# A decode layer on one core: the order of issue from a first pass that follows every operand, sample tokens and transposes as streams of their own, weight halves in two steps

## The chip, the cores and the metric

The kernel runs on one core of a Trainium2 chip. Such a core has a matrix engine (TensorE, "PE"), a vector engine (VectorE, "DVE"), a scalar engine (ScalarE, "ACT"), a general one (GpSimd, "POOL") and a queue for transfers (SyncE, "SP"). Each engine works through its own list of instructions in order; between engines they wait on semaphores. The metric is the device time of one execution in microseconds (us), the median of several runs.

## The reference

One layer of a hybrid decoder, in fp32, for 16 meta tokens and 256 prompt tokens of one sequence, and for 8 sample sequences of 4 tokens each that continue from stored states. Cut to its core:

```python
z = rms_norm(x, norm_mix) @ w_in                       # 2048 -> 3360 + 4096 columns
z_a, z_b = z[..., :RWKV_COLS], z[..., RWKV_COLS:]
o_a, S_a = rwkv7_mixer(z_a, shifted z_a, S_a0, ...)    # 16 heads of 64
o_b, S_b = retention_mixer(z_b, S_b0, pos, prompt)     # 4 heads of 256, chunks of 128
h = x + concat(o_a, o_b) @ w_out                       # 2048 -> 2048
hn = rms_norm(h, norm_ffn)
h = h + (silu(hn @ w_gate) * (hn @ w_up)) @ w_down     # 2048 -> 5632 -> 2048
y = rms_norm(h, norm_final)
```

Inside `rwkv7_mixer` each head runs a recurrence over the tokens:

```python
sa = einsum('bhij,bhj->bhi', S, a_t)
S = S * w_t[:, :, None, :] + sa[..., None] * b_t[:, :, None, :] + v_t[..., None] * k_t[:, :, None, :]
out = einsum('bhij,bhj->bhi', S, r_t)
```

Outputs are `y` for prompt and samples, and the new states.

## The kernel before

**Main work.** All weights lie in one array `big`, packed in the order of use, and come as tiles `wr` of 1024 columns (512 KB) over SP's queue, up to `WR` = 4 tiles ahead. A weight of fp32 is split on the chip in two halves of type fp32r: `halve` (line 540) lets ACT cast 512 columns to `wh` and DVE subtract it from the raw weight to give `wl`. For each block of 128x128 weights, `main` (line 552) issues three matmuls into one `acc` bank: `wh` with the activations' upper half `xh`, `wh` with their lower half `xl`, and `wl` with `xh`. One pair of halves thus feeds four such triples, 12 matmuls. There are two `acc` banks, and `WS` = 4 buffers for each half; halves are made up to three groups of 512 columns ahead of use. When a job's last matmul is issued, `evacuate` reads the bank. `main` runs through the projections of the RWKV pairs and retention heads, then out projection and FFN.

**Streams.** Beside `main` run generators that each stand for a chain of work, with a `yield` wherever the chain has to wait for another engine. For each of the 8 pairs of heads there is `pair` (line 817): decays, normalisation, the products of a unit of 64 tokens, then `inverse` (line 1000, it inverts a triangular matrix per unit), `units` (line 1080, the recurrence over the 5 units) and `pair_out`. Two smaller generators were stepped from within these: `by_token` (line 976, transposes of tiles to token-major form) inside `inverse`, and `sample` (line 1132, the tokens of the 8 sample sequences) inside `units`, each by a `next(other, None)` at places written out by hand. `ret` does a head of retention. All their matmuls go to the other six PSUM banks, named `mm`; all their scratch tiles lie in one SBUF array that the profile calls `arena_dt.float`.

`inverse` is a substitution in 15 rounds. A round s has one STREAM_SHUFFLE on DVE that spreads row s (tile `rs`, 128x80), and a multiply and an add on POOL over the columns that are left, 5 x (15 - s).

**What sets the order.** Every instruction goes through a proxy that books it with a planner (so nearly all rows of the profile have line 300). The planner keeps a clock for each engine and, for each stream, a time `ready`. It picks the first stream whose time has come, else one block of `main`:

```python
at = max(self.clock[eng], self.ready) + dur
self.clock[eng] = at
self.end = max(self.end, at + lat)
```

A stream's next step is ready when the last one, `end`, is over; what its operands wait for beyond that isn't followed. The kernel is built twice. The first pass (`draft`) notes when each scratch tile is used first and last, counted in instructions; `Room.place` (line 426) then packs them into the arena, so that a tile may take the place of one whose last use lies more than `slack` instructions back, with the largest slack of 40, 20, 10, 5, 0 that fits. The second pass decides the order anew and issues. After it, a compiler's scheduler may still move instructions of one engine past each other.

Of the kernel before, what the change touches and what calls it, by code (L numbers as in the profile page):

```python
# [304 lines left out]
class Plan:  # L305
# [4 lines left out]
    def __init__(self, nc, rooms, draft):  # L310
        self.rooms, self.draft, self.count = rooms, draft, 0
        self.clock = dict(PE=0.0, DVE=0.0, ACT=0.0, POOL=0.0)
        self.ready = self.end = 0.0
        self.mode, self.parts, self.empty, self.begun = None, {}, 0.0, 0.0
# [5 lines left out]
        self.sp = Timed(self, nc.sync, "SP")  # L320

    def book(self, eng, what, a, k):
        self.count += 1
        if self.draft:
            for x in (*a, *k.values()):
                for room in self.rooms.values():
                    room.use(x, self.count)
        if eng == "SP":
            return
        free = lambda ap: math.prod(ap.shape[1:])  # L330
        if eng == "PE":
            self.array(what, *a[:3])
            return
        else:
            n = free(a[0])
            fixed, per, lat = {"DVE": (60, 1.05, 100), "ACT": (190, 0.84, 150), "POOL": (100, 2.2, 100)}[eng]
            dur = fixed + per * n
        at = max(self.clock[eng], self.ready) + dur
        self.clock[eng] = at
        self.end = max(self.end, at + lat)  # L340

    def array(self, what, out, w, x):
# [4 lines left out]
        mode, part = (up(k), up(m)), (w.start_partition(), out.start_partition())  # L347
        if w.dtype == F32R:
            mode = up(k), 128
            dur = max(0.417 * n + 12, 107)  # L350
        elif what == "transpose":
            dur = max(0.83 * n + 4, 60)
        else:
            dur = 2 * max(0.833 * n + 3, 58 if m <= 64 else 110)
        if mode != self.mode:
            self.mode, self.parts, self.empty = mode, {}, self.clock["PE"] + 90
        at = max(self.parts.get(part, self.empty), self.ready, self.begun + 5)
# [3 lines left out]
        self.end = max(self.end, self.clock["PE"] + 250)  # L361
# [6 lines left out]
    def pick(self, now):  # L368

        return next((s for s in self.streams if s[2] <= now), None)  # L370

    def step(self, s):
        self.ready, self.end = s[2], s[2]
# [6 lines left out]
    def run(self, main):  # L380

        over = False
        while self.streams or not over:
            now = self.clock["PE"]
            s = self.pick(now)
            if s is None and not over:
                self.ready = self.end = 0.0
                try:
                    if next(main):
                        continue  # L390
                except StopIteration:
                    over = True
                    continue
            if s is None:
                assert self.streams, "nothing left to wait for"
                s = min(self.streams, key=lambda s: s[2])
            self.step(s)

    def finish(self, gen):

        self.ready = self.end = 0.0
        while True:
            try:
                next(gen)
                self.ready = self.end
            except StopIteration as e:
                return e.value
# [64 lines left out]
class Step:  # L472


    def __init__(self, tc, I, O, ctx, rooms, draft):
# [8 lines left out]
        self.n = 0  # L484
        self.plan = pl = Plan(self.nc, rooms, draft)
# [4 lines left out]
        self.pe, self.dve, self.act, self.pool = pl.pe, pl.dve, pl.act, pl.pool  # L490
        self.outs = []
# [7 lines left out]
    def flush(self, all=False):  # L499
        while self.outs and (all or self.outs[0][0] <= self.plan.clock["PE"]):  # L500
# [1175 lines left out]
```

## Time and profile before

| | us |
|---|---|
| median of 3 runs (lowest, highest) | 1585.04 (1582.96, 1585.89) |
| the profiled execution's own time | 1582.62 |
| its span, first to last instruction | 1580.8 |
| ACT casts `wh<-wr`, 826 of them, busy | 509.5 |
| DVE subtractions `wl<-wr,wh`, 826, busy | 571.3 |
| PE matmuls into `mm`, 1072, busy | 171.9 |
| waits of PE right before those | 19.3 |

The times are of one profiled execution. A busy time counts an engine's instructions without the gaps; a wait stands beside the instruction that came after it, with the engine and the tile that it was put down to. The page divides the span into 40 slices of 39.5 us; POOL is at work in the first 16 of them only, in which the streams run, and the clock granted to PE has its digit at 9 in all of them. Matmuls overlap in the pipeline, so that the duration of one in a row (300 to 390 ns) is longer than the distance from its start to the next one's.

### The profile page before, as it was taken

The page shows a single profiled execution, that of the slowest core. Times are in us where ns is not written, and L with a number is a line of the kernel's source. Part 1 is how long each engine was busy: PE and PEld are TensorE (multiplying, and loading weights), DVE is VectorE, ACT ScalarE, POOL GpSimd, SP SyncE. Part 2 cuts the span into 40 slices and gives each one's busy share as a digit, 9 for nine tenths or more (in the row PEclk, how much of TensorE's full clock was granted, in tenths as well). Part 3 has the DMA queues.
Part 4 walks back from the last instruction along what each step waited for, and adds up shares of the span by engine and source line. Part 5 has one row for each costly group of instructions (what it writes and reads, how often), then busy time and mean ns, then how long its engine had stood idle before and what let it go on. Part 6 is the DMA issues. An engine that isn't in the chain of part 4 may idle for free.

```text
span 1580.8 us, 30987 instructions
## 1 busy us (share of the span) xinstructions
PE 1544.1 (98%) x11388; PEld 1510.5 (96%) x11388; DVE 1125.7 (71%) x2590; ACT 842.7 (53%) x1795; POOL 182.5 (12%) x567
## 2 busy tenths in 40 slices
PE   9999999999999999999999999999999999999997
PEld 8989899998988989999999999999999999999997
DVE  7888789887997877776565656666666666565657
ACT  6756777577766556365444444444444444444445
POOL 1463314513143000000000000000000000000000
PEclk9999999999999999999999999999999999999999
DMA  7543344334544547755555555555555555555553
GB/s 280 152 126 108 102 121 138 118 102 126 181 131 139 168 161 231 241 162 160 166 167 165 169 163 171 162 171 161 169 165 166 168 163 171 162 172 162 169 163 114
DMA packets 77000, 252.50 MB, mean 160 GB/s; under 512 B 9392, under 2 KB 14640, under 8 KB 76848
## 3 DMA queue, kind: packets, MB, share of 16 engines
q1 hardware_dynamic: 76848, 250.52, 51.0%
q8 instruction: 90, 1.47, 0.4%
q14 instruction: 62, 0.51, 0.1%
HBM read 236.21 MB, written 14.28 MB: 158 GB/s over the span
## 4 chain that ended last, share of the span: by engine, by line
PE 68%; ACT 1%; DVE 1%; DMA 0%; issue 0%; POOL 0%; DVEq 0%; ACTq 0%; POOLq 0%
PE acc L300 64%; PE mm L300 4%; ACT arena_dt.float L300 1%; DVE arena_dt.float L300 1%; DMA arena_dt.float<-s0r 0%; DVE wl L300 0%; ACT wh L300 0%; ACT arena_dt.float32r L300 0%; POOL arena_dt.float L300 0%; DVEq L1672 0%; DVE arena_dt.float32r L300 0%; ACTq L300 0%; DVEq L300 0%; POOLq L300 0%
## 5 line engine op out<-in xcount | busy, mean ns | idle before, releaser
L300 ACT CAST wh<-wr 128x512 fp32r<-128x512 f32 x826 | 509.5, 619 | 577.4 <-PE acc L300 537.8
L300 PE MATMUL acc<-xh,wh 128*128 128x288 f32 (+2 forms) x2592 | 791.8, 305 | 0.5 <-ACT wh L300 0.3
L300 DVE TENSOR_TENSOR wl<-wr,wh 128x512 fp32r<-128x512 f32 x826 | 571.3, 693 | 282.2 <-ACT wh L300 259.9
L300 PE MATMUL acc<-xh,wl 128*128 128x288 f32 (+2 forms) x2592 | 771.3, 298 | 0.7 <-DVE wl L300 0.7
L300 PE MATMUL acc<-xl,wh 128*128 128x288 f32 (+2 forms) x2592 | 768.1, 296 | 0.0
L300 PEld LDWEIGHTS acc<-xh,wh 128*128 128x128 f32 x2592 | 488.3, 188 | 6.4 <-issue 2.7
L300 PEld LDWEIGHTS acc<-xl,wh 128*128 128x128 f32 x2592 | 487.5, 188 | 4.6 <-issue 1.4
L300 PEld LDWEIGHTS acc<-xh,wl 128*128 128x128 f32 x2592 | 486.9, 188 | 1.7 <-DVE wl L300 1.2
L300 PE MATMUL acc<-arena_dt.float32r,wh 128*128 128x288 f32 x1408 | 280.3, 295 | 0.0
L300 PEld LDWEIGHTS acc<-arena_dt.float32r,wh 128*128 128x128 f32 x1408 | 225.4, 188 | 0.3 <-ACT arena_dt.float32r L300 0.2
L300 PE MATMUL acc<-arena_dt.float32r,wl 128*128 128x288 f32 x704 | 206.8, 294 | 0.0
L300 PE MATMUL mm<-arena_dt.float 128*128 128x128 f32 (+8 forms) x1072 | 171.9, 320 | 19.3 <-DVE arena_dt.float L300 10.6
L300 PEld LDWEIGHTS mm<-arena_dt.float 128*128 128x128 f32 (+1 forms) x1072 | 140.2, 185 | 36.9 <-issue 10.5
L300 DVE TENSOR_TENSOR arena_dt.float<-arena_dt.float 128x288 f32<-128x288 f32 (+10 forms) x483 | 157.3, 351 | 11.1 <-ACT arena_dt.float L300 4.4
L300 DVE TENSOR_TENSOR arena_dt.float<-arena_dt.float,acc 128x288 f32<-128x288 f32 x208 | 94.3, 454 | 64.3 <-PE acc L300 63.8
L300 PEld LDWEIGHTS acc<-arena_dt.float32r,wl 128*128 128x128 f32 x704 | 132.8, 189 | 0.0
L300 ACT COPY arena_dt.float<-mm 64x64 f32<-64x64 f32 (+9 forms) x330 | 92.4, 287 | 53.0 <-PE mm L300 48.1
L300 ACT ACTIVATE arena_dt.float<-arena_dt.float 128x288 f32<-128x288 f32 (+6 forms) x200 | 85.3, 432 | 33.8 <-DVE arena_dt.float L300 28.0
L300 DVE TENSOR_TENSOR arena_dt.float<-acc,arena_dt.float 128x288 f32<-128x288 f32 (+4 forms) x181 | 72.9, 420 | 30.9 <-PE acc L300 30.4
L300 POOL TENSOR_TENSOR arena_dt.float<-arena_dt.float 128x70 f32<-128x70 f32 (+14 forms) x240 | 85.2, 356 | 62.0 <-DVE arena_dt.float L300 47.2
L300 POOL COPY arena_dt.float<-arena_dt.float 128x32 f32<-128x32 f32 (+5 forms) x123 | 43.9, 372 | 148.5 <-DVE arena_dt.float L300 81.6
L300 ACT COPY arena_dt.float<-arena_dt.float 64x320 f32<-64x320 f32 (+5 forms) x96 | 38.3, 412 | 16.5 <-POOL arena_dt.float L300 10.1
(64 smaller groups left out, 680.7 us busy)
## 6 DMA issues: line engine op xcount, KB each, us to landing
wr<-big SPq DMA_DIRECT2D x409, 512.0 KB, 3.5
arena_dt.float<-s0r SPq DMA_DIRECT2D x16, 512.0 KB, 4.5
out_rts<-arena_dt.float SPq DMA_DIRECT2D x16, 512.0 KB, 3.9
arena_dt.float<-xT SPq DMA_DIRECT2D x4, 576.0 KB, 5.1
out_y<-arena_dt.float SPq DMA_DIRECT2D x8, 288.0 KB, 2.2
arena_dt.float<-xT SPq DMA_DIRECT2D x7, 304.0 KB, 5.8
wr<-big SPq DMA_DIRECT2D x8, 256.0 KB, 5.6
arena_dt.float<-lora SPq DMA_DIRECT2D x16, 128.0 KB, 2.9
```

Of the source, the lines that this page charges most:

```text
L300: return f(*a, **k)
```

## The change

Each engine issues as many instructions of each kind as before. What differs is the order, some buffers, and where a few loads are issued.

1. **The planner.** In the first pass `book` looks at every operand of an instruction: it keeps, for each tile and each rectangle of it, when it is last written and read and by which engine, and starts the instruction no earlier than all of those that it depends on are done. Durations per engine and kind are finer, SP has a clock and a model of transfer times, and a tile that takes over a rotating buffer (`wr`, `wh`, `wl`, `acc`, `mm`) inherits the last use of its forerunner (`follows`). For a matmul the planner adds up how long PE would be held by operands that aren't there. Each choice of the first pass goes to `log`, and the second pass takes its choices from there.
2. **Streams of their own.** `by_token` and `sample` are added to the planner as streams, with the rank of their pair. `pair` waits for their ends where it needs them.
3. **`inverse` in three chunks.** Five shuffles go to one tile `rs` (128 x 5 x 80), then POOL does five rounds of multiply and add on it, three times.
4. **Memsets and copies in `pair`** stand earlier or in another order (`arp`, `bku`, `v0`, `ax`, `axd`).
5. **Loads.** `s0w` is issued with the first lora weights of its pair; `xT` (the residual, `ht`) one group of four tiles ahead of its use.
6. **Weight halves in two steps.** `cast` has the ACT part of `halve`; the subtraction, `rest`, follows in the middle of the group of 512 columns, or when its half is next.
7. **The scratch's limits.** The room for fp32r tiles is given as 4200 columns.

```diff
     def book(self, eng, what, a, k):
         self.count += 1
-        if self.draft:
...
+        if not self.draft:
             return
...
+        for name, box, writes in boxes:
+            for other, done, by, written in self.uses.get(name, ()):
+                if (written or writes) and done + 100 > at and not (by == eng == "PE") and meet(box, other):
+                    at = max(at, done + (30 if by == eng else 100 if eng == "PE" else 60))
...
     def run(self, main):
...
+            number = self.decide(lambda: self.pick(over or blocked))
+            blocked = False
+            if number:
+                self.step(next(s for s in self.streams if s[1] == number))
+                continue
...
-    def halve(self):
+    def cast(self):
...
         self.act.copy(hi, raw)
-        self.dve.tensor_sub(lo, raw, hi)
         self.halves.append((hi, lo))
+        self.rests.append((lo, raw, hi))
...
+    def rest(self):
+        for r in self.rests:
+            self.dve.tensor_sub(*r)
+        self.rests = []
...
                 while self.halved < min(total, at + (1 if starting else WS - 1) * 512):
-                    self.halve()
+                    self.cast()
                 hi, lo = self.halves.pop(0)
+                if self.rests and self.rests[0][0] is lo:
+                    self.rest()
+            if o == 256:
+                self.rest()
...
-        tok = self.by_token(v, v0, bku, bkt, sv, sav)
-        tt = yield from self.inverse(mt, tok)
+        self.plan.add(self.by_token(p, v, v0, bku, bkt, sv, sav), 1 + p)
+        self.plan.add(self.sample(p, v, ax, axd, bs, d4, s0), 1 + p)
+        tt = yield from self.inverse(mt)
+        while ("tok", p) not in self.done:
+            yield
...
-        for s in range(15):
-            rs = self.t([P, NU, 16], "rs")
-            dve.stream_shuffle(rs, rr, [16 * (i // 16) + s for i in range(32)])
-            if s % 4 == 3:
-                next(other, None)
-            yield
-            pool.tensor_mul(tm[:, :, s + 1:], rs[:, :, s + 1:], x[:, :, s:s + 1].to_broadcast([P, NU, 15 - s]))
...
-            yield
-            pool.tensor_add(x[:, :, s + 1:], x[:, :, s + 1:], tm[:, :, s + 1:])
...
+        for c in (0, 5), (5, 10), (10, 15):
+            rs = self.t([P, 5, NU, 16], "rs")
+            for s in range(*c):
+                dve.stream_shuffle(rs[:, s - c[0]], rr, [16 * (i // 16) + s for i in range(32)])
+            yield
+            for s in range(*c):
+                pool.tensor_mul(tm[:, :, s + 1:], rs[:, s - c[0], :, s + 1:],
+                                x[:, :, s:s + 1].to_broadcast([P, NU, 15 - s]))
+                pool.tensor_add(x[:, :, s + 1:], x[:, :, s + 1:], tm[:, :, s + 1:])
...
-    rooms[F32R].place(ROOM)
+    rooms[F32R].place(4200)
     rooms[F32].place(ROOM - rooms[F32R].size)
```

**What the packing makes of it.** Before, the fp32 arena had 28928 columns at a slack of 10 instructions; after, 28144 at a slack of 0 (with a slack of 5 it would need 29048, and 28952 are left). After, 191 of 982 takeovers of scratch columns come within ten issued instructions of the last use of the tile before; before, none did. In 65 of these 191 the last use is a read by PE, and the new tile is written by DVE (45), ACT (15) or POOL (5). Among the 16 handovers from one chunk's `rs` to the next one's, 8 put the new tile on columns of the one just read: first to second chunk in pairs 1, 2, 3 and 4, second to third in pairs 0, 3, 4 and 5. POOL reads the old chunk last with its ninth operation.

**Rows of PE, at a step of `units` of pair 1** (the one that PE waited longest for, 2.65 us, in the timeline of before). `mm_2378` is the product of one unit, `mm_2401` the transposes of `by_token` of pair 2, `mm_2405` the next product of the recurrence. Before:

```order
L300 MATMUL mm_2369<-arena_dt.float_70 128x128 x8
L300 MATMUL mm_2378<-arena_dt.float_70 128x128
L300 MATMUL acc_2348<-xh_72,wh_2281 128x304
L300 MATMUL acc_2348<-xl_73,wh_2281 128x304
L300 MATMUL acc_2348<-xh_72,wl_2282 128x304
L300 MATMUL mm_2401<-cst_262,arena_dt.float_70 128x128 x3
L300 MATMUL mm_2405<-arena_dt.float_70 128x128
```

After, from the same product (now `mm_2491`) to the same next one (`mm_2530`):

```order
L300 MATMUL mm_2491<-arena_dt.float_70 128x128
L300 MATMUL acc_2447<-xh_72,wh_2450 128x304
L300 MATMUL acc_2447<-xl_73,wh_2450 128x304
L300 MATMUL acc_2447<-xh_72,wl_2451 128x304
L300 MATMUL acc_2447<-xh_72,wh_2450 128x304
L300 MATMUL acc_2447<-xl_73,wh_2450 128x304
L300 MATMUL acc_2447<-xh_72,wl_2451 128x304
L300 MATMUL acc_2447<-xh_72,wh_2450 128x304
L300 MATMUL acc_2447<-xl_73,wh_2450 128x304
L300 MATMUL acc_2447<-xh_72,wl_2451 128x304
L300 MATMUL acc_2447<-xh_72,wh_2450 128x304
L300 MATMUL acc_2447<-xl_73,wh_2450 128x304
```

The twelfth `acc` matmul and `mm_2530` follow. Between the two products stood one triple and three transposes; now four triples stand there, and the transposes are elsewhere.

**Rows of DVE, at the shuffles of pair 2's `inverse`.** Before; the rows with `mm_2378` are the state update of `units` that PE's 2.65 us wait was for, the shuffle ahead of them belongs to `inverse`:

```order
L300 STREAM_SHUFFLE arena_dt.float_70<-arena_dt.float_70 128x80 x2
L300 TENSOR_TENSOR arena_dt.float_70<-arena_dt.float_70 128x48
L300 STREAM_SHUFFLE arena_dt.float_70<-arena_dt.float_70 128x80
L300 TENSOR_TENSOR arena_dt.float_70<-arena_dt.float_70 128x8x2x3
L300 TENSOR_TENSOR arena_dt.float_70<-arena_dt.float_70,cst_262 128x256
L300 STREAM_SHUFFLE arena_dt.float_70<-arena_dt.float_70 128x80
L300 SCALAR_TENSOR_TENSOR arena_dt.float_70<-mm_2378,arena_dt.float_70 64x64 x2
```

After; the first five shuffles are chunk one, the ten are chunks two and three, the `wl` are subtractions of weight halves:

```order
L300 STREAM_SHUFFLE arena_dt.float_70<-arena_dt.float_70 128x80 x5
L300 TENSOR_TENSOR arena_dt.float_70<-arena_dt.float_70 128x288
L300 STREAM_SHUFFLE arena_dt.float_70<-arena_dt.float_70 128x80 x10
L300 TENSOR_TENSOR wl_2402<-wr_2204,wh_2401 128x512
L300 TENSOR_TENSOR wl_2451<-wr_2204,wh_2450 128x512
L300 TENSOR_TENSOR arena_dt.float_70<-acc_2279,arena_dt.float_70 128x304
L300 TENSOR_TENSOR arena_dt.float_70<-arena_dt.float_70 128x288
```

Between two rounds' shuffles stood operations of other streams; now all fifteen stand within two rows, with one operation of 128x288 between chunk one and the rest, and two subtractions behind them.

More of the change, by code (lines that the diff above doesn't have):

```diff
@@ L338, in book @@
[L338 to L342, printed above, removed]
+        if not self.draft:
+            return
+        aps = [x for x in (*a, *k.values()) if hasattr(x, "shape")]
+        for x in aps:
+            for room in self.rooms.values():
+                room.use(x, self.count)
+        out, ins = aps[0], aps[1:]
+        at = 0.0
+        boxes = [(x.name, self.box(x), x is out) for x in aps if x.name not in self.outside]
@@ L345, in array @@
+        for name, box, writes in boxes:
+            uses = self.uses.setdefault(name, [])
+            if writes:
+                uses[:] = [u for u in uses if not (box[0] <= u[0][0] and u[0][1] <= box[1] and box[2] <= u[0][2]
+                                                   and u[0][3] <= box[3])]
+            uses.append((box, done, eng, writes))
+        self.end = max(self.end, done + 100)
+    def array(self, what, out, w, x, ready):
         n, m, k = math.prod(x.shape[1:]), math.prod(w.shape[1:]), w.shape[0]
@@ L366, in add, with pick @@
         self.streams.sort(key=lambda s: s[:2])
-    def pick(self, now):
-        return next((s for s in self.streams if s[2] <= now), None)
+    def pick(self, over):
+        now = self.clock["PE"]
+        s = next((s for s in self.streams if s[2] <= now), None)
+        if s is None and over:
+            assert self.streams, "nothing left to wait for"
+            s = min(self.streams, key=lambda s: s[2])
+        return s[1] if s else 0
     def step(self, s):
-        self.ready, self.end = s[2], s[2]
+        self.end = s[2]
         try:
@@ L380, in run @@
     def run(self, main):
-        over = False
+        over = blocked = False
         while self.streams or not over:
[L384 to L402, printed above, removed]
-            try:
[L404 to L407, printed above, removed]
+            number = self.decide(lambda: self.pick(over or blocked))
[3 more added lines that the diff above has]
+                continue
+            try:
+                blocked = not next(main)
+            except StopIteration:
+                over = True
 class Room:
@@ L499, in flush @@
     def flush(self, all=False):
-        while self.outs and (all or self.outs[0][0] <= self.plan.clock["PE"]):
+        due = lambda: sum(all or at <= self.plan.clock["PE"] for at, _, _ in self.outs)
+        for _ in range(self.plan.decide(due)):
             _, dst, src = self.outs.pop(0)
@@ L821, in pair @@
             yield
-        while not all(("lora", i) in self.done for i in range(3)) or len(z) < 4:
+        while not all(("lora", i) in self.done for i in range(3)) or len(z) < 5:
             yield
```

187 lines of the change are left out of this document (114 added, 73 removed).

## The prediction

> **What bounds the kernel now.** I read the page's table of engines first, then busy time by stage.
>
> ```profile
> PE 1544.1 (98%) x11388; PEld 1510.5 (96%) x11388; DVE 1125.7 (71%) x2590; ACT 842.7 (53%) x1795; POOL 182.5 (12%) x567
> ```
>
> ```profile
> 25.00:640.00 615.00, 591.71 (x4230) 561.45 (x4229) 510.90 (x1511) 399.83 (x1024) 177.97 (x536) 0.99 0.45 144
> 640.00:1560.00 920.00, 919.78 (x6945) 918.94 (x6945) 583.86 (x1016) 416.25 (x723) 0.00 (x0) 1.00 0.55 167
> 1560.00:1580.80 20.80, 10.22 (x83) 9.89 (x81) 13.22 (x31) 6.14 (x12) 0.00 (x0) 0.82 0.29 115
> ```
>
> The columns of the last three rows are the stretch, its length, then PE, PEld, DVE, ACT and POOL busy, granted PE clock, DMA share and GB/s. TensorE (PE) sets the end. From 640 us on it waits 0.2 us in 920, so nothing can be won there while it stays fed. The last 20.8 us are a serial chain (final norm) that the change leaves in its order. What is left is the stage from 25 to 640 us, where the projections run as filler beside the RWKV and retention streams: PE is idle there for 615.00 - 591.71 = 23.3 us. The waits of PE in that stage, longest sums first (engine, tile, what was waited for, us, times, longest):
>
> ```profile
> PE mm L300 <- DVE arena_dt.float L300: 10.6, 9, 2.6
> PE mm L300 <- ACT arena_dt.float L300: 9.8, 5, 3.8
> PE mm L300 <- POOL arena_dt.float L300: 0.8, 1, 0.8
> PE acc L300 <- DVE wl L300: 0.7, 1, 0.7
> PE mm L300 <- DMA arena_dt.float<-s0r: 0.4, 1, 0.4
> PE acc L300 <- ACT wh L300: 0.3, 1, 0.3
> ```
>
> 18 waits give 22.6 us, and nearly all stand before `mm` matmuls, those of the streams. Two of them close up. First the timeline of PE (start, busy us, operation, in brackets the wait ahead of it and what ended it):
>
> ```profile
> 115.93 0.29 PE L300 MATMUL acc<-xh,wl 128*128 128x288 f32 x1
> 120.03 1.30 PE L300 MATMUL mm<-arena_dt.float 128*128 128x64 f32 x5 [3.80 <-ACT arena_dt.float L300]
> ...
> 185.84 0.46 PE L300 MATMUL mm<-arena_dt.float 128*128 128x128 f32 x2 [2.65 <-DVE arena_dt.float L300]
> ```
>
> Then, for the wait that ends at 120 us, the timelines of POOL and of ACT:
>
> ```profile
> 115.20 3.83 POOL L300 TENSOR_TENSOR arena_dt.float<-arena_dt.float 128x70 f32<-128x70 f32 x8
> ```
>
> ```profile
> 118.69 0.56 ACT L300 ACTIVATE arena_dt.float<-arena_dt.float,pv 128x312 f32<-128x312 f32 x1 [3.03 <-POOL arena_dt.float L300]
> ```
>
> And for the one at 185 us that of DVE:
>
> ```profile
> 184.96 0.01 DVE L300 LOAD_MASK_SELECT arena_dt.float<-arena_dt.float  x1 [2.36 <-POOL arena_dt.float L300]
> 184.96 0.24 DVE L300 STREAM_SHUFFLE arena_dt.float<-arena_dt.float 128x80 f32<-128x80 f32 x1
> 185.11 0.59 DVE L300 SCALAR_TENSOR_TENSOR arena_dt.float<-mm,arena_dt.float 64x64 f32<-64x64 f32 x2
> ```
>
> At 120 us ACT's head waits 3.03 us for POOL, which is in a run of eight operations of `inverse`, and PE waits 3.80 us for ACT. At 185 us the recurrence (`units`) needs a DVE operation (at 185.11) that stands in the queue behind a shuffle of another pair's `inverse`; that shuffle's mask load waits 2.36 us for POOL, and PE, in order too, waits 2.65 us. So these are not long chains: **they are heads of in-order queues that wait for POOL, with a stream's next step behind them.**
>
> A wait costs more than its row. From start to start at 115.93 there are 4.10 us; 3.80 are booked and one pitch is 40 us / 304 = 0.13 us by this row,
>
> ```profile
> 1000.00:1040.00 40.00, 40.00 (x304) 40.00 (x303) 26.40 (x46) 17.00 (x29) 0.00 (x0) 1.00 0.54 164
> ```
>
> so 0.17 us of drain are booked as busy, 18 x 0.17 = 3.1 us in all. And the granted clock falls behind some waits:
>
> ```profile
> 118.00:128.00 10.00, 7.97 (x42) 8.00 (x43) 4.95 (x19) 3.60 (x9) 1.92 (x8) 0.66 0.32 102
> 304.00:316.00 12.00, 10.17 (x67) 9.95 (x66) 9.56 (x34) 5.64 (x14) 4.68 (x15) 0.86 0.31 99
> 364.00:374.00 10.00, 7.42 (x43) 6.71 (x43) 5.89 (x28) 4.91 (x14) 4.48 (x19) 0.83 0.40 129
> 500.00:512.00 12.00, 9.58 (x73) 6.85 (x72) 7.90 (x42) 7.77 (x22) 7.54 (x27) 0.86 0.15 59
> ```
>
> Lost clock is (1 - 0.66) x 10 = 3.4, then 0.14 x 12, 0.17 x 10 and 0.14 x 12 = 1.7 each: 8.5 us. The stage thus loses 23.3 + 3.1 + 8.5 = **34.9 us**, which is what a perfect order could give. (Gaps too short to be booked may add some; no row shows them.)
>
> The Trainium skill, "TensorE: Matmul & The Clock Gate", Part 1, says that the array falls to half rate after about 3.4 us without work, in a free-running window. The trace agrees on the half rate, not on the length: the window at 304 holds a wait of 1.8 us only.
>
> ```profile
> PE mm L300 <- DVE arena_dt.float L300: 1.8, 1, 1.8
> ```
>
> **The change part by part.** Instruction counts per engine are equal; only order, DMA times and buffers move.
>
> *Order.* The first pass now books every operand, so a stream's matmul is placed where its inputs should be done. In the rows of PE in the change's section, the `units` matmul of the 2.65 us wait had one triple of `acc` matmuls and three transposes behind the previous one, 6 x 0.13 = 0.8 us of cover; it now has four triples, 12 x 0.13 = 1.6 us. The same holds for the other `units` and `inverse` steps that I compared: a step that was waited for has 0.8 to 1.5 us in the old order and mostly 1.2 to 3.3 us in the new one (triples counted, 0.4 us each). The samples' stream no longer sits inside `units`, so the pair's last two `units` groups no longer wait for it. If every wait went, 34.9 us would go. Cover of 1.6 us doesn't hide a queue whose head is stuck for 2 to 4 us, so I price the stuck heads apart.
>
> *Inverse in chunks.* Same 15 shuffles, 30 POOL operations and 2 masks per pair; what goes is the hop between DVE and POOL in each of 15 rounds. What comes is a new wait: the scratch packing has slack 0, and in 8 of 16 handovers the next five shuffles write the columns that POOL's last chunk still reads. DVE's head then waits until POOL's ninth operation. POOL's run of 8 takes 3.83 us, 0.48 each, at 70 columns; at 25 columns it is 1.17 / 4 = 0.29:
>
> ```profile
> 101.58 1.17 POOL L300 TENSOR_TENSOR arena_dt.float<-arena_dt.float 128x25 f32<-128x25 f32 x4
> ```
>
> First-to-second handovers (4) hold DVE for 9 x 0.48 = 4.3 us, second-to-third (4, 50 to 30 columns, midway 0.385) for 3.5 us. Queued behind are weight halves: in the rows of DVE for pair 2, ten shuffles stand ahead of two `wl`. PE notices once the halves in stock are used: between a half's subtraction and its first use stand some 20 matmuls now (two chunks of 12 less the six that `rest` comes later, and two), 20 x 0.13 = 2.6 us; before it was 26, 3.4 us. Left for PE: 4 x (4.3 - 2.6) + 4 x (3.5 - 2.6) = **10.4 us**. From below it is zero, if DVE reaches the shuffles late enough; from above the whole hold, 4 x 4.3 + 4 x 3.5 = 31 us. I take the middle since a stuck head of 2.36 us gave 2.65 us at 185 us but DVE's waits for POOL in the stage,
>
> ```profile
> DVE arena_dt.float L300 <- POOL arena_dt.float L300: 15.8, 21, 2.4
> ```
>
> 21 of them, gave few waits of PE that long. *Clock:* four of the six waits of 1.8 us or more were followed by lost clock at 1.7 us or more; the new waits are just below 1.8, so I keep two, 3.4 us.
>
> *Weight halves in two steps.* 826 casts and 826 subtractions as before; the subtraction comes six matmuls later. Behind 640 us DVE is busy 583.86 of 920 us and the stock of 2.6 us covers a subtraction of 0.68 us: nothing. If that cover failed, each chunk of 12 matmuls could cost up to 0.68 us, in the stage's 230 chunks too; no row points to it.
>
> *DMAs moved.* `s0w` is issued with the lora weights, `xT` four columns of tiles earlier:
>
> ```profile
> arena_dt.float<-xT SPq DMA_DIRECT2D x4, 576.0 KB, 5.1
> ...
> arena_dt.float<-s0w SPq DMA_DIRECT2D x8, 256.0 KB, 3.8
> ```
>
> On SP's queue they are moved past loads of `wr`. Of these up to four tiles are loaded ahead (`WR`), each 24 matmuls long, 24 x 0.13 = 3.1 us of PE, so one issue more in between doesn't make a weight late; and the eight and four loads land before their first reader in both orders. I take nothing; above, the 0.4 us that PE waits for `s0r` could grow by one landing, 3.8 us. *More reuse:* 191 of 982 scratch tiles now take columns read within the ten instructions before, none did; 65 of these pairs make DVE, ACT or POOL wait for PE's last read. One such wait is at most a pitch or two, and PE runs ahead of the three there; zero to 65 x 0.2 = 13 us. I take zero, as PE's read is the earlier one in the order.
>
> *Sum:* 34.9 - 10.4 - 3.4 = 21.1 us off the profiled execution's 1582.62, that is 1561.5; the runs' median, 1585.04, is 2.4 above it, so **1564**.
>
> **The rivals.** *Nearly all of it comes:* DVE arrives at the shuffles when POOL is done, and the covers hold. For it: POOL is busy 177.97 of 615 us only. Then 1585 - 35 = 1550, or 1546 with the unbooked gaps.
>
> *The order doesn't hold:* the compiler's scheduler moves instructions after the planner, on DVE more than on any other engine, and the rows of pair 2 show it: shuffles ahead of older `wl`. With DVE busy 510.90 of 615 us, 83%, delays don't drain and new waits of the old size form: 1577 to 1588, no change to speak of.
>
> *Slower:* the same eight holds at their full price. If POOL's runs lengthen to 0.6 us an operation, a hold is 9 x 0.6 = 5.4 us, and ten shuffles (0.15 us each from start to start at 184.96, 1.5 us) stand before the first `wl`; less the stock of 2.6 us that is 4.3 us for PE, and 1.7 us of clock each: 8 x 6.0 = 48 us against 34.9 won, 1598. It decides in the `inverse` of pairs 0 to 5, as soon as a hold costs PE over 34.9 / 8 - 1.7 = 2.7 us. Against it: half of the holds are the shorter kind.
> The Trainium skill, "SBUF — State Buffer", section "Who interferes with whom", has a rule for it: a DVE operation with two SBUF inputs and a GpSimd operation that reads SBUF lock each other out for a whole instruction. By it nine operations could each wait for one subtraction of 0.68 us, 9 x (0.48 + 0.68) = 10 us. Two subtractions that fell into the run of eight took 0.76 and 0.78 us instead of 0.68, so the trace shows a tenth of that:
>
> ```profile
> 99.72 0.68 DVE L300 TENSOR_TENSOR wl<-wr,wh 128x512 fp32r<-128x512 f32 x1
> ...
> 115.86 0.78 DVE L300 TENSOR_TENSOR wl<-wr,wh 128x512 fp32r<-128x512 f32 x1
> ...
> 116.99 0.76 DVE L300 TENSOR_TENSOR wl<-wr,wh 128x512 fp32r<-128x512 f32 x1
> ```
>
> **How the numbers follow.** Forecast (1555 to 1575): 0.52. Nearly all: 0.28. Order doesn't hold: 0.12, half of it within 0.2% (3.2 us, about what a measurement of this kernel tells from no change), a third faster. Slower: 0.08. So faster 0.52 + 0.28 + 0.04 = 0.84, same 0.06, slower 0.10. The range takes in the whole gain and most of the third case: 1546 to 1582.
>
> **What would show it.** PE's waits in the stage should fall from 22.6 us to about 10 to 14, with few over 2 us; windows with clock under 0.9 from four to two. DVE's waits for POOL should rise from 15.8 us to some 30, with shuffles or their mask load at the head; if they fall, the holds were nothing and the gain is larger. Waits of `acc` for `wl`, 0.7 us before, should grow to several us. PE from 640 us on must stay full, or the two-step halves cost. Wrong altogether if waits for `mm` stay near 20 us.

## The result and the profile after

The changed kernel took 1604.03 us (median; 1600.69 to 1606.78), the one before on the same chip 1584.09: a ratio of 1.0124, 95% interval 1.0102 to 1.0146. Forecast were 1564 us; it is slower by 20 us, outside the range given.

Busy time by stage of the changed kernel (the same columns and stretches as before):

```profile
25.00:640.00 615.00, 574.92 (x4040) 545.54 (x4038) 495.82 (x1482) 386.47 (x1001) 183.34 (x544) 0.97 0.43 135
640.00:1560.00 920.00, 920.00 (x6955) 917.86 (x6955) 578.94 (x1006) 410.12 (x711) 0.00 (x0) 1.00 0.56 170
```

Behind 640 us PE is as full as it was. In the streams' stage it is idle for 40.1 us in place of 23.3. The waits of PE there (tile, what was waited for, sum, times, longest):

```profile
PE mm L300 <- DVE arena_dt.float L300: 13.3, 7, 4.7
PE mm L300 <- ACT arena_dt.float L300: 11.1, 12, 3.9
PE mm L300 <- DMA arena_dt.float<-s0r: 8.7, 3, 6.8
PE acc L300 <- DVE wl L300: 6.5, 3, 3.3
```

These are 39.6 us in 25 waits, where there were 22.6 in 18: 17.0 us more, and 7 x 0.17 = 1.2 us of drain. The granted clock fell in seven places:

```profile
92.00:100.00 8.00, 5.54 (x29) 5.55 (x30) 7.61 (x22) 2.72 (x5) 5.09 (x16) 0.79 0.22 79
132.00:140.00 8.00, 4.11 (x20) 3.88 (x19) 4.60 (x20) 5.31 (x14) 5.03 (x17) 0.79 0.23 67
196.00:204.00 8.00, 6.29 (x36) 6.33 (x37) 6.40 (x22) 4.30 (x11) 1.25 (x6) 0.79 0.55 164
348.00:356.00 8.00, 8.00 (x45) 7.50 (x45) 4.14 (x11) 2.90 (x8) 0.32 (x2) 0.79 0.18 67
396.00:404.00 8.00, 8.00 (x45) 6.84 (x36) 1.72 (x4) 2.15 (x9) 0.37 (x2) 0.57 0.00 1
484.00:492.00 8.00, 4.93 (x29) 3.98 (x30) 2.08 (x5) 1.23 (x3) 0.00 (x0) 0.57 0.55 185
540.00:548.00 8.00, 5.12 (x23) 4.87 (x23) 5.73 (x17) 2.39 (x7) 0.88 (x4) 0.68 0.30 104
```

That is 8 x (4 x 0.21 + 2 x 0.43 + 0.32) = 16.2 us of lost clock, 7.7 more than before. 17.0 + 1.2 + 7.7 = 25.9 us, beside a span that is 1605.0 - 1580.8 = 24.2 us longer (one execution each): the loss lies in these waits and the clock behind them.

Three of the longest, each with the head that was stuck behind it. First the timelines of PE and DVE around 197 us:

```profile
197.71 0.46 PE L300 MATMUL mm<-arena_dt.float 128*128 128x128 f32 x2 [4.72 <-DVE arena_dt.float L300]
```

```profile
193.85 0.42 DVE L300 TENSOR_TENSOR arena_dt.float<-arena_dt.float,cst 128x256 f32<-128x256 f32 x1 [2.64 <-POOL arena_dt.float L300]
...
197.00 0.56 DVE L300 SCALAR_TENSOR_TENSOR arena_dt.float<-mm,arena_dt.float 64x64 f32<-64x64 f32 x2
```

PE waits for the state update of `units` (at 197.00), which stands in DVE's queue behind a masked product `em` of another pair's `inverse` (at 193.85). By the packing `em` takes over columns of the last `rs`, which POOL is still reading. It is the same picture as at 185 us before; only the operation at the head is another one. Its wait is 2.64 of the 4.72 us; other operations of DVE's queue follow between the two.

Then ACT's and POOL's timelines for the wait of 3.89 us that ends at 136.78:

```profile
133.51 0.46 ACT L300 ACTIVATE arena_dt.float<-arena_dt.float 128x312 f32<-128x312 f32 x1 [3.84 <-POOL arena_dt.float L300]
```

```profile
125.20 9.27 POOL L300 TENSOR_TENSOR arena_dt.float<-arena_dt.float 128x75 f32<-128x75 f32 x20 [0.24 <-DVE arena_dt.float L300]
```

By the packing the tile of 312 columns, of pair 2, lies on an `rs` of pair 1's `inverse`; ACT, which also serves `units` and the casts, stands until POOL has read it.

Last, POOL's and SP's timelines ahead of the longest wait, 6.79 us for `s0r`:

```profile
466.26 13.80 POOL L300 TENSOR_TENSOR arena_dt.float<-arena_dt.float 128x75 f32<-128x75 f32 x30 [2.60 <-DVE arena_dt.float L300]
480.00 0.56 POOL L300 COPY shout<-arena_dt.float 128x1 f32<-128x1 f32 x2
```

```profile
474.02 0.33 SPq L300 DMA_DIRECT2D wr<-big  x1
480.59 0.34 SPq L300 DMA_DIRECT2D out_sh<-shout  x1
481.02 0.89 SPq L300 DMA_DIRECT2D arena_dt.float<-s0r  x2
```

```profile
487.07 2.04 PE L300 MATMUL mm<-arena_dt.float 128*32 128x256 f32 x16 [6.79 <-DMA arena_dt.float<-s0r]
```

All 30 operations of one `inverse` stand in a block of 13.80 us on POOL. Two small copies into `shout` queue behind it; SP's head, the output of `shout`, waits for those; and two loads of `s0r` that PE needs queue behind that. What the three have in common is POOL's block. (This last chain is read from the trace; no run took it away by itself, but e3, e6 and e7 below say more of it.)

### The profile page after: what moved, and what is told of

Read it like the earlier page. It is cut to its first block, busy times and chain, and to the rows that moved or that the text cites. A ratio compares the mean times of both kernels' runs of the same rounds, so it can differ in the third digit from the quotient of the medians.

```text
span 1605.0 us, 31012 instructions
## 1 busy us (share of the span) xinstructions
PE 1552.0 (97%) x11388; PEld 1518.1 (95%) x11388; DVE 1125.4 (70%) x2590; ACT 841.2 (52%) x1795; POOL 186.5 (12%) x567
## 4 chain that ended last, share of the span: by engine, by line
PE 66%; DVE 1%; ACT 0%; issue 0%; POOL 0%; DVEq 0%; POOLq 0%
PE acc L300 63%; PE mm L300 3%; DVE arena_dt.float L300 1%; ACT arena_dt.float L300 0%; DVE wl L300 0%; POOL arena_dt.float L300 0%; DVEq L1740 0%; ACT wh L300 0%; DVEq L300 0%; POOLq L300 0%
## 5 line engine op out<-in xcount | busy, mean ns | idle before, releaser
L300 PE MATMUL mm<-arena_dt.float 128*128 128x128 f32 (+6 forms) x1072 | 175.3, 320 | 31.5 <-DVE arena_dt.float L300 13.3
L300 DVE TENSOR_TENSOR arena_dt.float<-arena_dt.float 128x288 f32<-128x288 f32 (+11 forms) x483 | 158.0, 354 | 11.7 <-ACT arena_dt.float L300 6.2
L300 POOL TENSOR_TENSOR arena_dt.float<-arena_dt.float 128x75 f32<-128x75 f32 (+14 forms) x240 | 81.4, 339 | 61.1 <-DVE arena_dt.float L300 36.7
L300 POOL COPY arena_dt.float<-arena_dt.float 128x32 f32<-128x32 f32 (+4 forms) x123 | 45.3, 384 | 102.0 <-DVE arena_dt.float L300 49.4
L300 POOL MEMSET arena_dt.float<- 128x64 f32 (+8 forms) x137 | 30.9, 238 | 184.4 <-DVE arena_dt.float L300 82.3
```

What stands on the lines that cost most here:

```text
L300: return f(*a, **k)
```

## The experiments

All ratios are against the kernel before, run beside each; "us" is the ratio less one, times 1583.

| run | edit | median us | ratio (95% interval) | us |
|---|---|---|---|---|
| the change | | 1604.03 | 1.0124 (1.0102 to 1.0146) | +19.6 |
| e1 | change, every engine in the planner's order | 1594.96 | 1.0072 (1.0049 to 1.0094) | +11.4 |
| e2 | before, every engine in the planner's order | 1687.38 | 1.0654 (1.0627 to 1.0682) | +103.5 |
| e3 | change, 15 rounds | 1573.51 | 0.9937 (0.9916 to 0.9958) | -10.0 |
| e4 | change, halves in one step | 1591.03 | 1.0054 (1.0038 to 1.0071) | +8.5 |
| e5 | change, POOL's columns kept 80 instructions | 1597.12 | 1.0091 (1.0072 to 1.0109) | +14.4 |
| e6 | change, slack 20 | 1601.26 | 1.0124 (1.0103 to 1.0145) | +19.6 |
| e7 | 15 rounds, slack 0 | 1580.38 | 0.9986 (0.9977 to 0.9996) | -2.2 |
| e8 | change, yield behind each round | 1584.98 | 1.0015 (1.0005 to 1.0026) | +2.4 |
| e9 | change, one step, order untouched | 1598.90 | 1.0116 (1.0096 to 1.0136) | +18.4 |
| e10 | 15 rounds, one step, order untouched | 1574.39 | 0.9954 (0.9939 to 0.9969) | -7.3 |
| e11 | 15 rounds, POOL and SP in planner's order | 1581.64 | 0.9993 (0.9981 to 1.0004) | -1.1 |
| e12 | before, with the chunks | 1612.62 | 1.0199 (1.0184 to 1.0214) | +31.5 |
| e13 | change, `em` ahead of the chunks | 1590.67 | 1.0051 (1.0036 to 1.0066) | +8.1 |
| e14 | change, chunks of 3 | 1590.22 | 1.0048 (1.0033 to 1.0063) | +7.6 |
| e15 | 15 rounds, slack 40 | 1575.78 | 0.9961 (0.9950 to 0.9973) | -6.2 |
| e16 | e13, readers held back | 1578.41 | 0.9971 (0.9958 to 0.9984) | -4.6 |
| e17 | 15 rounds, readers held back | 1567.71 | 0.9899 (0.9882 to 0.9917) | -16.0 |
| e18 | change, readers held back | 1588.18 | 1.0036 (1.0025 to 1.0048) | +5.7 |

**e1 and e2: the order as planned.** Each recorded instruction is tied behind the one issued before it on its engine:

```diff
-            return f(*a, **k)
+            r = f(*a, **k)
+            if not self._plan.draft:
+                self._plan.tc.keep_in_program_order(r)
+            return r
```

> The changed kernel, with every engine's instructions kept in the order in which the planner issued them, so that the compiler's scheduler can't move one past another. Theory A (the scheduler brings instructions forward to places where their scratch columns are still being read, and the heads of POOL, DVE and ACT wait there): the 39.6 us of PE's waits in 25 to 640 us fall under 15 us and the time to 1555 to 1575 us. Theory B (the blocks of POOL operations in the inverse are what stands in the way, in any order): 1595 us or more, with waits above 30 us. Theory C (the stock of weight halves is too small): also 1595 or more, with waits for wl of 6 us or more.

> The kernel before with every engine's instructions kept in the planner's order. Theory A says that the old planner's order was itself poor, since it didn't follow operands, and needed the scheduler: 1585 or slower, up to 1620. If keeping the order helps whatever planner stands behind it, 1565 to 1580.

The change gained 8 us by it, far from what theory A wanted: its waits of PE became many small ones, and POOL's block stayed. In the row of its waits for `wl`:

```profile
PE acc L300 <- DVE wl L300: 11.9, 18, 1.3
```

So theory A falls for the change; what theory B wanted, 1595 us or more with waits above 30 us, came within 0.04 us (1594.96, with 32.1 us of waits). The kernel before lost 103 us, far beyond what was expected: the new planner's order can stand alone, the old one's can't. Taking away the scheduler's freedom as a whole wins back 8 of the change's 20 us; which of its moves do harm, e18 asks below.

**e3: no chunks.** The old loop of 15 rounds comes back. The two masked products `em` come back into it as well (at `s` = 8 and 12, as in the kernel before); the chunks had moved them behind the last one. All else stays:

```diff
-        for c in (0, 5), (5, 10), (10, 15):
-            rs = self.t([P, 5, NU, 16], "rs")
...
+        for s in range(15):
+            rs = self.t([P, NU, 16], "rs")
+            dve.stream_shuffle(rs, rr, [16 * (i // 16) + s for i in range(32)])
+            yield
...
```

> The changed kernel with the inverse in its 15 rounds as before (one shuffle, one multiply, one add, and so on), all else as changed. Theory B (blocks on POOL and the handovers of rs): most of the loss goes, 1575 to 1588. Theory A: the scheduler still moves the rest, 1590 to 1605. Theory C: 1600 to 1605.

Better than any theory had it: 30 us less than the changed kernel and 10 us less than before. But the smaller tiles also gave the packing a slack of 20 in place of 0, so e6 and e7 had to follow.

**e4, e9 and e10: the halves.** In e4 `cast` calls `rest` at once; in e9 and e10 only the second pass does, so that planner and packing see the same as before:

```diff
         self.rests.append((lo, raw, hi))
+        if not self.draft:
+            self.rest()
```

> The changed kernel with the subtraction of a weight half issued right behind its cast, as before. Theory C: the 6.5 us of waits for wl and some clock go, 1590 to 1597. Theories A and B: within 4 us of the changed kernel, 1600 to 1606.

> The changed kernel with its planner's order and its packing untouched; only the subtraction of each weight half is issued right behind its cast again. Theory C (the two steps take stock from PE, which the blocks of shuffles then use up): the 6.5 us of waits for wl go and with them their clock, 1592 to 1599. If the two steps cost nothing, as the prediction had it: 1601 to 1606.

> The same for the changed kernel with the inverse in 15 rounds (1573.5 us, with 0.2 us of waits for wl): nothing is left to win from the halves there, 1571 to 1576.

e4 looked like a gain of 11 us from the halves, but there the planner had chosen another order and the packing another slack (20). With the order untouched (e9, e10) nothing is left beyond the intervals: 1.0116 against 1.0124, and 0.9954 against 0.9937. e9's median, 1598.90, does lie in theory C's range, but the kernel before was faster beside it too (1581.47), and 5.4 of the 6.5 us of waits for `wl` are still there. The two steps cost nothing that these intervals show, and theory C falls. e4's gain is that of another order and packing, and shows that these alone can move this kernel by 11 us: a difference of that size between runs with different orders proves little.

**e5, e6, e7 and e15: early reuse of scratch.** In e5, in the packing, a tile's end is put off by its last use on POOL:

```diff
-            b += slack
+            b = max(b + slack, self.pool.get(i, 0) + 80)
```

In e6 and e15 three weight tiles (in the second pass) in place of four leave 1024 columns more; e7 is e3 with only a slack of 0 to choose.

> The changed kernel in the planner's unchanged order; only the packing of the scratch differs: a column that POOL has read or written isn't given to another tile until 80 instructions later. Theory D (the loss is DVE, ACT and SP waiting for POOL's last read of a column that they take over, as at 133.5 and 193.9 us): 1585 to 1592. Theory B (the blocks of ten to thirty POOL operations hold up what is queued behind them on POOL itself, reuse or not): 1597 to 1605.

> The changed kernel with room for a slack of 20 instructions in the packing, as against 0; the room comes from the weight tiles, three in place of four. Theory D in its wide form (all early reuse, whatever the engine): 1580 to 1588. Theory B: 1595 to 1605. If three weight tiles are too few, PE waits for wr or wh from 640 us on, which nothing showed before.

> The changed kernel with the inverse in 15 rounds, packed at a slack of 0 as the changed kernel was; the run with 15 rounds before this one had a slack of 20 and gave 1573.5. Theory B: still 1572 to 1580. Theory D in its wide form: most of the gain is lost, 1588 to 1604.

> The changed kernel with the inverse in 15 rounds and room for a slack of 40 (three weight tiles in place of four). From 0 to 20 it went from 1580.4 to 1573.5; if reuse still costs something at 20, 1567 to 1573, else 1573 to 1577.

With chunks, a slack of 20 gave nothing (1.0124 both times; the three weight tiles kept PE full behind 640 us, 919.99 us of 920), the longer hold of POOL's columns about 5 us, with intervals that overlap. Without chunks, a slack of 0 cost 0.49% or 7.8 us against 20, and 40 was no better than 20. At equal slack the chunks cost 21.8 us (the change against e7, both at 0) and 29.6 us (e6 against e3, both at 20); the planner's order differs within each pair, but both differences are well beyond e4's 11 us. So reuse is the smaller part, and the chunks cost by themselves. In e6 the longest of DVE's waits for POOL is now at the first readers of the inverse's result (DVE's timeline); masked products still wait 2.6 and 2.3 us in two places (a block of 30 operations is longer than a slack of 20):

```profile
374.44 0.73 DVE L300 TENSOR_TENSOR arena_dt.float<-arena_dt.float,cst 128x160 f32<-128x160 f32 x2 [6.20 <-POOL arena_dt.float L300]
```

The chain by way of `shout` stands in e6 too (POOL's and SP's timelines), and PE waits 3.6 us for `s0r` behind it:

```profile
461.37 8.80 POOL L300 TENSOR_TENSOR arena_dt.float<-arena_dt.float 128x55 f32<-128x55 f32 x22
```

```profile
470.60 0.34 SPq L300 DMA_DIRECT2D out_sh<-shout  x1
471.03 0.38 SPq L300 DMA_DIRECT2D arena_dt.float<-s0r  x1
```

In e3 PE doesn't wait for `s0r` at all. But e7, with 15 rounds and a slack of 0, has 6.4 us of such waits in two places, with no output of `shout` ahead of those loads: POOL's block is not their only cause, and the other wasn't followed.

**e8 and e14: shorter blocks.** e8 puts a yield behind each round of multiply and add; e14 has five chunks of three.

```diff
                 pool.tensor_add(x[:, :, s + 1:], x[:, :, s + 1:], tm[:, :, s + 1:])
+                yield
```

> The changed kernel with the shuffles in chunks of five, but a yield behind each round of POOL's multiply and add, so that the planner can put other work of POOL between the rounds; the packing has a slack of 10. Theory B: 1575 to 1588, POOL's longest run of operations without another in between well below 13.8 us. Theory D: about what a slack of 10 brings, 1590 to 1598.

> The changed kernel with five chunks of three rounds in place of three of five; the packing has a slack of 20. Theory B goes by the length of POOL's blocks: between 15 rounds (1573.5) and three chunks at a slack of 20 (1601.3), 1580 to 1595. If it is only a matter of chunks or no chunks: 1598 to 1604.

Both times fit theory B: at a slack of 20, chunks of one, three and five rounds gave -10.0, +7.6 and +19.6 us (the second step, 12 us, is hardly more than another order moved in e4); with yields the chunks of five cost 17 us less. But the sign that theory B gave for e8, a longest run of POOL well below 13.8 us, didn't come. POOL's timelines of e8 and, for comparison, of e3, the longest run of each:

```profile
301.23 11.53 POOL L300 TENSOR_TENSOR arena_dt.float<-arena_dt.float 128x75 f32<-128x75 f32 x30
```

```profile
182.44 4.84 POOL L300 TENSOR_TENSOR arena_dt.float<-arena_dt.float 128x70 f32<-128x70 f32 x10 [0.56 <-DVE arena_dt.float L300]
```

A run of 30 stands in e14 as well (12.50 us, from 517.47). A yield lets other work in between, and nothing makes it come. As e8's slack (10) and order differ too, it stays open what its 17 us come from.

**e11 and e12.** e11 keeps POOL and SP, in e3's kernel, in the planner's order; e12 puts the chunks alone into the kernel before.

> The changed kernel with the inverse in 15 rounds, and POOL's and SP's instructions kept in the order in which the planner issued them, so that no memset stands early at POOL's head and waits there for a column to come free. Theory A for what is left of the waits: 1560 to 1570. If POOL's order matters only where it has long blocks: 1571 to 1577.

> The kernel before with one part of the change alone: the inverse's shuffles in three chunks of five and POOL's ten operations behind each (the transposes are stepped once per chunk). Theory B: slower than before by 10 to 30 us, 1593 to 1613, whatever the planner. If the chunks cost only together with the new planner: 1580 to 1588.

e11 missed both expectations: it lost 9 us against e3. That memsets stand early at POOL's head is thus not shown to hurt; why keeping POOL's order costs wasn't followed further. In e12 **the chunks cost the kernel before 31 us**, under the old planner as under the new. Two things come with them there: `em` moves behind the last chunk, and the packing falls to a slack of 0 (28160 columns), where the kernel before has 10.

**e13, e16, e17 and e18: the readers.** e13 makes the masked products `em`, which don't need the inverse, ahead of the loop. e16 to e18 keep DVE's first readers of the result, `xm` (128x160) and `tt` (128x320), and in e18 also `em`, behind the twelve DVE instructions that were issued before them, by order alone and without a wait:

```diff
-        dve.tensor_mul(xm.rearrange("p u (q c) -> p u q c", c=16), x[:, :, None, :].to_broadcast([P, NU, 2, 16]),
+        self.hold(dve.tensor_mul, xm.rearrange("p u (q c) -> p u q c", c=16), x[:, :, None, :].to_broadcast([P, NU, 2, 16]),
...
+    def hold(self, f, *a):
+        r = f(*a)
+        if not self.draft:
...
+            for i in same[-12:]:
+                self.tc.add_manual_dep(r.ins, i.name, dep, reason="hold")
```

> The changed kernel with the two masked products em of the inverse made ahead of the chunks in place of behind them (the packing then has a slack of 20). In the changed kernel em stood at DVE's head at 139.4, 193.9, 323.3 and 540.5 us, waiting 1.1 to 2.6 us for POOL's last chunk. Theory D (heads that wait for POOL's last read of a column): with these and the reuse gone, 1580 to 1590. Theory B (whatever is behind the block comes late, and what needs the inverse's result still stands early on DVE): 1593 to 1602.

> The run with em ahead of the chunks (1590.7 us), and the two multiplications on DVE that first read the inverse's result (128x160 and 128x320) kept behind the twelve DVE instructions that the planner issued before them. In that run they stood at DVE's head and waited 3.4, 2.5 and 3.3 us for POOL. Theory B in the form that the readers of a long block stand too early on DVE: DVE's waits for POOL fall from 11.4 us to under 5 and the time to 1578 to 1586. If the block does its harm on POOL itself: 1588 to 1593.

> The changed kernel with the inverse in 15 rounds (1573.5 us) and the same two multiplications held back. DVE waited 6.3 us for POOL there, at most 1.3 at once, so little is left to win: 1569 to 1575.

> The changed kernel with its planner's order and its packing (slack 0) untouched; only em and the two first readers of the inverse's result, all on DVE, are kept behind the twelve DVE instructions that the planner issued before them. If these readers standing early on DVE are most of what the chunks cost: 1578 to 1590, DVE's waits for POOL falling from 28.5 us to about 12, what the handovers of rs leave. If reuse and the block on POOL are the larger part: 1594 to 1604.

e13 came out between the two theories. In e18 four multiplications per pair of the changed kernel are tied, and no other line is edited: it is 14 us faster (1.0124 to 1.0036), within the first of the two ranges. In the changed kernel about half of these 32 stood further ahead in DVE's list than the planner had put them, by up to 35 places. DVE's waits for POOL fell to 17.3 us, not to about 12: those at the tied readers went from 10.2 to 0.9 us, those at shuffles only from 16.9 to 15.6:

```profile
DVE arena_dt.float L300 <- POOL arena_dt.float L300: 17.3, 25, 3.0
```

DVE's timeline at the place of the 4.72 us wait now reads

```profile
194.79 0.59 DVE L300 SCALAR_TENSOR_TENSOR arena_dt.float<-mm,arena_dt.float 64x64 f32<-64x64 f32 x2
...
199.24 0.59 DVE L300 SCALAR_TENSOR_TENSOR arena_dt.float<-mm,arena_dt.float 64x64 f32<-64x64 f32 x2
199.87 0.76 DVE L300 TENSOR_TENSOR arena_dt.float<-arena_dt.float,cst 128x256 f32<-128x256 f32 x2
```

`em` stands behind two state updates, and PE waits 1.65 us there. What e18 keeps are the holds on ACT and on POOL's own queue, and shuffles that wait for POOL's reads of `rs` (PE's timeline):

```profile
95.02 0.41 PE L300 MATMUL acc<-xh,wl 128*128 128x304 f32 x1 [3.28 <-DVE wl L300]
...
137.83 0.80 PE L300 MATMUL mm<-arena_dt.float 128*128 128x128 f32 x2 [3.89 <-ACT arena_dt.float L300]
...
472.89 2.05 PE L300 MATMUL mm<-arena_dt.float 128*32 128x256 f32 x16 [6.57 <-DMA arena_dt.float<-s0r]
```

In e16, with `em` ahead as well, the changed kernel with its chunks is no longer slower than the kernel before, and DVE hardly waits for POOL in the stage (the row of DVE's waits; 28.5 us in the changed kernel):

```profile
DVE arena_dt.float L300 <- POOL arena_dt.float L300: 0.2, 1, 0.2
```

e17, better than expected, beats the kernel before by 1.0% (0.8 to 1.2), and by its ratio the changed one by 2.2%: the new planner, the streams, 15 rounds and held readers. Its stage and its waits of PE:

```profile
25.00:640.00 615.00, 598.36 (x4325) 568.43 (x4324) 524.25 (x1536) 402.14 (x1034) 185.25 (x540) 1.00 0.47 150
```

```profile
PE mm L300 <- ACT arena_dt.float L300: 8.2, 14, 1.5
PE mm L300 <- DVE arena_dt.float L300: 6.3, 9, 1.5
PE mm L300 <- issue: 0.8, 1, 0.8
PE acc L300 <- ACT wh L300: 0.7, 1, 0.7
PE acc L300 <- DVE wl L300: 0.2, 1, 0.2
```

No wait is over 1.5 us, and the clock holds.

Four runs at a slack of 20 make a ladder: the chunks as they are +19.6 us (e6), `em` ahead of them +8.1 (e13), the readers held too -4.6 (e16), 15 rounds with held readers -16.0 (e17). So `em`'s place, the readers' place and the block itself come to some 11 to 13 us each. Only the middle step leaves the planner's order untouched; the other two carry the uncertainty that e4 showed.

## Why the prediction was wrong, step by step

**What bounds the kernel: right.** Heads of in-order queues that wait for POOL, with a stream's step behind them, were what PE waited for before, and are so after, with more of them.

**Order: right in sign, and the largest error in size.** The step "if every wait went, 34.9 us would go" took the ceiling for the term. Without the chunks all the rest of the change brought 10 us with a slack of 20 (e3), and 2 us with the change's own slack of 0 (e7). PE's waits in e3 are 19.5 us in 27 pieces, where the kernel before had 22.6 in 18: the new order made the waits shorter, and more of them. What the pieces that are left hang on wasn't followed. With this term as it came and the chunks as they were priced, the sum would have come out some 4 us slower than before: this term alone was enough to leave the range.

**Inverse in chunks: the step that failed, and turned the sign.** It was priced at 10.4 us for PE and 3.4 us of clock; it cost 21.8 us at equal slack (e7 against the change), and some 30 with the slack that its larger tiles take (e3 against the change; e12). The sum counted one kind of hold, of a chunk's shuffles at DVE's head. Four such of over 1.3 us stood in DVE's timeline, not eight, and shorter than the 3.5 to 4.3 us of the sum:

```profile
89.63 0.01 DVE L300 LOAD_MASK_SELECT arena_dt.float<-arena_dt.float  x1 [2.10 <-POOL arena_dt.float L300]
...
263.27 0.01 DVE L300 LOAD_MASK_SELECT arena_dt.float<-arena_dt.float  x1 [1.74 <-POOL arena_dt.float L300]
...
318.69 0.01 DVE L300 LOAD_MASK_SELECT arena_dt.float<-arena_dt.float  x1 [1.49 <-POOL arena_dt.float L300]
...
372.42 0.01 DVE L300 LOAD_MASK_SELECT arena_dt.float<-arena_dt.float  x1 [2.99 <-POOL arena_dt.float L300]
```

What it left out is what else waits for a block of 10 to 30 operations on one queue: the readers of its result and the masked products behind it, placed early on DVE (14 us, e18); a tile of another pair that takes the block's columns, on ACT; and what queues behind the block on POOL itself, down to SP's loads. These last two are read from the trace, and no run prices them. The 15 hops between DVE and POOL, which the prediction saw only as something that goes, had kept POOL's runs shorter: at most 8.41 us in the kernel before and 4.84 in e3, 13.80 in the change.

The row that the prediction named did show it, DVE's waits for POOL in the stage:

```profile
DVE arena_dt.float L300 <- POOL arena_dt.float L300: 28.5, 30, 3.1
```

That is "some 30" as said, and the waits of `acc` for `wl` grew to 6.5 us as said. But the agreement of the 28.5 is in part luck: 16.9 us of it stand at shuffles, in 22 pieces (8.3 at the four above), and 10.2 at five masked products and first readers, which the sum didn't have. By its other sign, that waits for `mm` near 20 us would make it wrong altogether, the forecast was refuted: they came to 33.1 us. The clock, with two lost windows kept in the sum (3.4 us), fell in seven (16.2 us).

**Halves in two steps: right**, nothing (e9, e10). **DMAs: wrong by their place.** The moved `s0w` and `xT` cost nothing seen, but PE's waits for `s0r` grew from 0.4 to 8.7 us; in the longest, 6.8 us, the output of `shout` stood ahead of the loads at SP's head. **More reuse, taken as zero** within 0 to 13 us: nothing with chunks (e6), 7.8 us without (e7), so the bound held and the value didn't.

**The rival "slower"** came out at 1598, near what was measured, by a neighbouring mechanism, and got 0.08. That its number is so near is luck: it charged eight full holds by shuffles, and four shorter ones came, beside heads that it didn't have. Its argument against ("half of the holds are the shorter kind") weighed the sizes of the holds that were counted, not the queues that weren't looked at.

**The rule on DVE and GpSimd.** The prediction set aside the rule of the Trainium skill, "SBUF — State Buffer", section "Who interferes with whom", since DVE's subtractions beside POOL's run took only 0.76 to 0.78 us. That looked at the wrong engine: the one that stretches here is POOL. Here is the same operation of `inverse` on 128x45 in POOL's timeline, first beside a subtraction of `wl`, then beside a shuffle, each with its neighbour from DVE's:

```profile
471.98 0.73 POOL L300 TENSOR_TENSOR arena_dt.float<-arena_dt.float 128x45 f32<-128x45 f32 x1
```

```profile
471.89 0.68 DVE L300 TENSOR_TENSOR wl<-wr,wh 128x512 fp32r<-128x512 f32 x1
```

```profile
373.17 0.29 POOL L300 TENSOR_TENSOR arena_dt.float<-arena_dt.float 128x45 f32<-128x45 f32 x1
```

```profile
373.13 0.24 DVE L300 STREAM_SHUFFLE arena_dt.float<-arena_dt.float 128x80 f32<-128x80 f32 x1
```

By that rule of the Trainium skill a shuffle, with one input, doesn't hold POOL and a subtraction with two does; these rows agree. So do all 240 such operations of the changed kernel: the 104 that overlapped a TENSOR_TENSOR of DVE with both inputs in SBUF took 0.43 us in the mean, the other 136 took 0.27, and the former are longer in each of the 15 shapes. The 826 subtractions hardly changed: 0.71 us in the mean where they met one of these, 0.69 elsewhere.

## What to carry to other kernels

Before you join many small steps into one block to save hops, list for the engine that runs the block all that is queued behind it and all that reads its result or takes its memory on other queues; each of those is a head that can hold a stream. A reader that an order of issue puts early on an in-order queue can hold it until the block ends (6.20 us at once in e6), and tying such readers behind a few older instructions, without any wait, was worth 14 us here (e18), more than the rest of the change without the chunks (10 us, e3). Try an edit with the order of everything else untouched (e9), or its effect can't be told from that of another order (e4). When an edit changes the size of a tile, compare at the same packing (e7), or what the lost room costs is taken for what the edit costs.

## What the runs showed of the hardware that was not expected

A block of 30 POOL operations has no fixed length. Here are the stretches of two such blocks of the changed kernel, of the same 30 operations each (after the length: PE, PEld, DVE, ACT, POOL busy):

```profile
466.30:480.00 13.70, 13.70 (x99) 12.06 (x97) 11.95 (x56) 12.55 (x31) 11.43 (x30) 1.00 0.44 133
368.20:378.40 10.20, 9.04 (x62) 8.10 (x60) 2.77 (x21) 9.93 (x33) 7.93 (x30) 1.00 0.42 131
```

With DVE busy for 11.95 us POOL's operations took 11.43 us in all, with DVE mostly stuck (2.77 us) 7.93. A planner that books POOL at one price misses by 44% between these two (11.43 / 7.93).

And the clock: in the window from 348 us it fell to 0.79, and the longest wait of PE ahead of that was

```profile
347.84 1.43 PE L300 MATMUL mm<-arena_dt.float 128*128 128x128 f32 x7 [2.25 <-DVE arena_dt.float L300]
```

so that a wait of 2.25 us was enough, as one of 1.8 us had been in the kernel before. The length of the wait doesn't decide alone. The clock of 0.57 from 396 us on followed two waits of about 1 us close together:

```profile
393.51 1.04 PE L300 MATMUL mm<-arena_dt.float 128*32 128x256 f32 x6 [0.80 <-DMA arena_dt.float<-s0r]
395.65 1.54 PE L300 MATMUL mm<-arena_dt.float 128*32 128x256 f32 x12 [1.09 <-DMA arena_dt.float<-s0r]
```

In the kernel before, longer ones, of 2.65 us at 185 us and of 2.95 us at 462 us, were followed by a clock of 1.00. What decides is open.
